# One square root for the head norms of two chunks, and the gate's tanh traced next to the decay's, in an RWKV-7 and Conformer step

## The chip, the cores and the metric

The kernel runs on one core of one Trainium2 chip, in one launch. Its time is device time in microseconds (us). Of the core's engines five appear here: TensorE (PE in the profile, with PEld for its weight loads) multiplies matrices, VectorE (DVE) and ScalarE (ACT) work element by element, GpSimd (POOL) does the same and issues transfers, SyncE (SP) issues transfers.

## The reference

One step of a hybrid decoder of two layers over 16 meta tokens, 1024 prompt tokens and 8 decode tokens (1048 columns), 1024 features wide. Layer 0 mixes tokens by a causal Conformer convolution, layer 1 by RWKV-7 with 16 heads of 64; each is followed by a squared-ReLU MLP of 4096. The change lies in layer 1. Cut to what matters:

```python
def _rwkv7(h, shift_prev, S0, x_mix, ...):
    ...
    r = xr @ w_r; k = xk @ w_k; v = xv @ w_v
    w_log = -softplus(-(w0 + tanh(xw @ w1) @ w2)) - 0.5
    decay = exp(-exp(w_log))
    a = sigmoid((a0 + (xa @ a1) @ a2))
    g = sigmoid(xg @ g1) @ g2
    kk = k * k_k;  kk = kk / max(sqrt(sum(kk * kk, per head)), L2_EPS)
    ...
    S_final, ys = lax.scan(_wkv7_step, S0, xs)
    y = moveaxis(ys, 0, 1)
    mu = mean(y, per head)
    var = mean(square(y - mu), per head)
    yn = (y - mu) * rsqrt(var + GN_EPS)
    yn = yn * gn_g + gn_b
    bonus = sum(r * k * r_k, per head) * v
    out = ((yn + bonus) * g) @ w_o
```

## The kernel before

Features lie on the 128 partitions in eight blocks, tokens along the free axis. Layer 0 and its MLP come first. Layer 1's mixer runs over four groups of tokens (`G1`: 272, 256, 256 and 264 columns). `mixer_in(g, tick)` loops over the eight feature blocks p (each of two heads): the projection r, the gate's second matrix, the decay and a (a tanh of each), the projection v, then a scan and products on DVE that make the operands of the recurrence. Ahead of the loop stand two narrow matmuls for the group: `gate` (tile lg, sigmoid written as a tanh) and, at p = 0, `decay_rate` (tile lwa).

The recurrence itself goes over 17 chunks of 64 tokens, the first of them the meta tokens. `front(c)` makes the products of a chunk (tiles A, nr, no), `chunk(c)` goes on with gg, bT, W, U, S and Y; Y is copied to a tile `ey`. `inverses` solves small triangular systems on DVE in many short steps (tiles tt and ni, one pair of instructions a step). All this is fed in between the projections: at each call of `tick` the generators of the inverses, of the recurrence and of `norm_gate` advance by a step.

`norm_gate` is the function that the change is about. It takes chunks in pairs (c, c + 1), c = 1, 3, ..., 15. For each chunk `stats` normalises 64 tokens x 16 heads, which lie as 128 partitions x 8 heads x 64: sum over a head (DVE, `ems`), centring (DVE), Square (ACT, `eq`), sum (DVE), Sqrt of 128x8 (ACT), reciprocal (DVE), and the multiplication of `ey` (DVE, 128x512). With a `yield` between, these are spread over ticks. Then, for each half of the features, PE transposes the pair (`yn`), ACT applies scale and bias (`ez`), DVE adds the bonus (`ebv`) and multiplies by the gate (`egt`), and the result is stored to a scratch `d_z`. At the end the 8 decode rows go the same way in two halves (`eyd`, `emsd`, `ynd`).

The Sqrt needs another table of functions in ACT than Tanh and Exp, so an `ACT_TABLE_LOAD` stands in ACT's queue wherever one follows the other. The key norms (`r16f`, one Sqrt a group) and the norms of the MLP layers are square roots as well.

What sets the order: each engine's instructions are put in order by a scheduler that simulates a timeline, with the code's order as the priority. PE is excepted in the mixer and in the tail: it keeps the order of the code. So are single instructions wrapped in `kept_place`, which keep their place among such on their engine.

After the mixer three tail groups (`G2`: 328, 352 and 352 columns) read `d_z`, multiply by w_o (`mixer_out`) and run layer 1's MLP (matmuls `ps_in` and `out`, additions to `h`) and the last norm. The first of them runs while the last chunks, the decode step and their norms are still being fed in.

Of the kernel before, what the change touches and what calls it, by code (L numbers as in the profile page):

```python
# [11 lines left out]
AF = mybir.ActivationFunctionType  # L12
ALU = mybir.AluOpType
AX = mybir.AxisListType
PSUM = bass.MemoryType.PSUM

P = 128
D = 1024
KT = D // P
# [3 lines left out]
DEC = 8  # L23
# [4 lines left out]
HS = 64  # L28
# [18 lines left out]
def hybrid_step(tc, x_prompt, x_sample, state_conv, state_shift, state_wkv, meta_tokens,  # L47
# [8 lines left out]
    nc = tc.nc  # L56
    ctx = ExitStack()
    with ctx:
# [8 lines left out]
        eps_t = consts.tile([P, 4], F32, name="eps_t")  # L67
# [39 lines left out]
        for name, ap in vecs:  # L107
            n = ap.shape[0]
# [28 lines left out]
        kept_place = tc.keep_in_program_order  # L137
# [258 lines left out]
        with ExitStack() as l0:  # L396
# [16 lines left out]
            h = {}  # L413
# [341 lines left out]
        for i, op in enumerate((ALU.is_gt, ALU.is_ge)):  # L755
            v = m_ar[:HS, i * HS:(i + 1) * HS]
# [210 lines left out]
        def mixer_in(g, tick):  # L967

            c0, n = G1[g]
# [42 lines left out]
            lg = lorap.tile([P, N1], F32, name=nm("lg"), tag="lg")  # L1012

            def decay_rate(ws):
                ps = narrow(ws, "wa")
                nc.scalar.activation(lwa[HALF[0], :n], ps[HALF[0]], AF.Tanh)
                nc.scalar.copy(lwa[HALF[1], :n], ps[HALF[1]])

            def gate(ws):
                ps = bank(nm("p", "g"))[:, :n]  # L1020
                for k in range(KT):
                    nc.tensor.matmul(ps, ws[k // HK][:, k % HK, :], mix(5, k), start=k == 0, stop=k == KT - 1)
                nc.scalar.activation(lg[:, :n], ps, AF.Tanh, scale=0.5)
                nc.scalar.activation(lg[:, :n], lg[:, :n], AF.Copy, scale=0.5, bias=0.5)

            def lora2(w, p, act, name):
                ps = bank(nm("l2", name))
# [15 lines left out]
            lumps = g == 2  # L1043
            spaced = (lambda: None) if lumps else both
            wg, ww = gate_w(), rate_w()
            gate(wg)
            act = mixed(0)
            carry["tail"]()
            act_v = mixed(3)
# [66 lines left out]
            for p in range(KT):  # L1116
                if p:
                    spaced()
                ps = proj(next(wrkv), act, n, nm("r", p), *((spaced, (3,)) if p else (first,)))
                rk2 = pr.tile([P, 2, N1], F32, name=nm("rk2", p), tag="rk2", bufs=2)  # L1120
                nc.scalar.copy(rk2[:, 1, :n], ps[:, :n])
                if p == 0:
                    decay_rate(ww)
                if g < 3:
                    for _ in keys_amid(p):
# [3 lines left out]
                ps = lora2(wg2, p, lg, f"g{p}")  # L1129
# [16 lines left out]
                ps = proj(next(wrkv), act_v, n, nm("v", p), spaced, (3,))  # L1146
# [114 lines left out]
        n_ = lambda shape, name, c, tag=None, bufs=1: wn.tile(shape, F32, name=f"{name}{c}", tag=tag or name, bufs=bufs)  # L1261
# [237 lines left out]
        def norm_gate():  # L1499

            KH = KT // 2
            fm = lambda t, n: t[:, :KH * n].rearrange("p (k t) -> p k t", k=KH)

            def stats(y, n, name):

                yv = y[:n].rearrange("t (h v) -> t h v", v=HS)
                ms = n_([P, 2, KT], "ems", name)
                sq = n_([P, KT * HS], "eq", name)
                over = lambda j: ms[:n, j].unsqueeze(2).broadcast_to([n, KT, HS])
                nc.vector.tensor_reduce(ms[:n, 0], yv, axis=AX.X, op=ALU.add)  # L1510
                nc.vector.scalar_tensor_tensor(yv, over(0), -1.0 / HS, yv, op0=ALU.mult, op1=ALU.add)
                yield 1
                kept_place(nc.scalar.activation(sq[:n], y[:n], AF.Square))
                yield 1
                kept_place(nc.vector.tensor_reduce(ms[:n, 1], sq[:n].rearrange("t (h v) -> t h v", v=HS), axis=AX.X, op=ALU.add))
                yield 1
                kept_place(nc.scalar.activation(ms[:n, 1], ms[:n, 1], AF.Sqrt, scale=1.0 / HS, bias=eps_t[:n, 2:3]))
                yield 1
                kept_place(nc.vector.reciprocal(ms[:n, 1], ms[:n, 1]))
                nc.vector.tensor_mul(yv, yv, over(1))  # L1520

            def load_rest(hf, lo, n):

                two = [n_([P, KH * P], tag, f"{lo}_{hf}", bufs=b) for tag, b in (("ebv", 1), ("egt", 2))]
                for t, src in zip(two, (d_bv, d_g)):
                    nc.sync.dma_start(fm(t, n), src[:, hf * KH:(hf + 1) * KH, lo:lo + n])
                return two

            def gated(pt, hf, lo, n, bv, gt):

                z = n_([P, KH * P], "ez", f"{lo}_{hf}", "eq")
                yield 0.5
                for k in range(KH):
                    p = hf * KH + k
                    kept_place(nc.scalar.activation(z[:, k * n:(k + 1) * n], pt[:, k * n:(k + 1) * n], AF.Identity, scale=vec("gn_g", p), bias=vec("gn_b", p)))
                w = KH * n
                yield 1
                kept_place(nc.vector.tensor_add(bv[:, :w], z[:, :w], bv[:, :w]))
                nc.vector.tensor_mul(gt[:, :w], bv[:, :w], gt[:, :w])
                yield 1  # L1540
                kept_place(nc.sync.dma_start(d_z[:, hf * KH:(hf + 1) * KH, lo:lo + n], fm(gt, n)))

            for c in range(1, NCH, 2):
                for i in range(2):
                    while st["done"] < c + i:
                        yield 1
                    yield from stats(ys[c + i], P, c + i)
                lo = META + (c - 1) * HS
                for hf in range(2):
                    rest = load_rest(hf, lo, P)  # L1550
                    yield 3
                    if not hf:
                        yield 1
                        yield 1
                    pt = bank(f"yn{c}_{hf}", "w")
                    to = pt.rearrange("p (j a u t) -> p j a u t", a=2, u=2, t=HS)
                    for j in range(2):
                        for i in range(2):
                            nc.tensor.transpose(to[:, j, :, i, :], ys[c + i][:, (2 * hf + j) * P:(2 * hf + j + 1) * P], ident)
                    yield from gated(pt, hf, lo, P, *rest)  # L1560
                st["free"] = c + 1
                st["normed"] = c + 1
            while not st["decoded"]:
                yield 1
            y8 = [n_([P, KT * HS], "ey", f"d{hf}", bufs=3) for hf in range(2)]
            for hf in range(2):
                nc.sync.dma_start(y8[hf][:DEC], d_y[:, hf * KH * P:(hf + 1) * KH * P])
            rest = load_rest(0, NP_TOK, DEC)
            yield 4
            for hf in range(2):  # L1570
                yield from stats(y8[hf], DEC, f"d{hf}")
            for hf in range(2):
                if hf:
                    rest = load_rest(hf, NP_TOK, DEC)
                    yield 3
                pt = bank(f"ynd_{hf}", "w")
                for k in range(KH):
                    nc.tensor.transpose(pt[:, k * DEC:(k + 1) * DEC], y8[hf][:DEC, k * P:(k + 1) * P], ident[:DEC, :DEC])
                yield from gated(pt, hf, NP_TOK, DEC, *rest)
            st["normed"] = NCH  # L1580
# [220 lines left out]
```

## Time and profile before

| | before |
|---|---|
| runs | 2641.32, 2638.36, 2640.5 us; median 2640.5 |
| the profiled execution | 2641.17 us, its span 2639.5 us |
| mean granted clock of TensorE | 0.993 |
| ACT_TABLE_LOAD of the head norms (L1517) | 9, of 1283 ns |
| ACT_TABLE_LOAD of the blocks' tanh (L1144) | 6, of 1283 ns |
| ACT_TABLE_LOAD of the key norms (L958) and of the decay's tanh (L1016) | 4 and 4, of 1283 ns |
| ACT_TABLE_LOAD of the gate's tanh (L1023) | 3, of 1283 ns |

The profile is of one execution. A row of the timeline gives the start and the duration in us, engine, line, operation, the tiles out<-in, and in brackets how long the engine idled before it and what ended that. A row of the groups gives the busy time and the mean duration in ns, then the idle time before and its releaser. A row of the windows gives a stretch, its length, the busy time of PE, PEld, DVE, ACT and POOL in it (with the instructions), the granted clock of TensorE (1.00 is full speed), and the DMA engines' busy share and GB/s. In the span, the gates' tanh of the four groups start from 1115.4 to 1550.4 us, the reciprocals of the head norms from 1376.0 to 1912.8, those of the decode rows at 2058.7 and 2064.5.

### The profile page before, as it was taken

The numbers are of one execution on the slowest core, as the hardware profiler recorded it, in microseconds if no ns is written. First come the engines' busy times: TensorE is split into PE (matmuls) and PEld (weight loads), VectorE is DVE, ScalarE is ACT, GpSimd is POOL, SyncE is SP. The second block draws the span as 40 slices with busy tenths as digits, with TensorE's granted clock in tenths as the row PEclk, the third lists the DMA queues.
The fourth block names the chain that finished last, engine by engine and source line by source line (L and its number), as shares of the span: only waits on it lengthen the run. The fifth ranks groups of instructions, "written<-read, shape, count | busy, mean of one in ns | idle before, by whom it ended". The sixth has DMA issues, their size and how long they took to land.

```text
span 2639.5 us, 51709 instructions
## 1 busy us (share of the span) xinstructions
PE 2584.5 (98%) x19956; PEld 2439.1 (92%) x19956; DVE 1720.5 (65%) x3610; ACT 1129.0 (43%) x2093; POOL 1453.0 (55%) x2060
## 2 busy tenths in 40 slices
PE   9999999999999999999999999999999999999998
PEld 8999999999999999877787877799999999999998
DVE  6999999997544444544867567686689544444435
ACT  5546435444534333233344545555444542222223
POOL 7677878878878777122111213476588763333331
PEclk9999999999999999999999999999999999999999
DMA  6663544554446543678876867898575542222211
GB/s 189 174 164 111 163 142 132 161 171 137 142 137 179 157 137 119 181 202 205 227 191 191 217 170 189 217 206 195 149 215 174 147 132 68 69 72 64 73 49 45
DMA packets 602060, 400.24 MB, mean 152 GB/s; under 512 B 96128, under 2 KB 548928, under 8 KB 601814
## 3 DMA queue, kind: packets, MB, share of 16 engines
q1 hardware_dynamic: 573764, 360.08, 49.7%
q0 software_dynamic: 8720, 26.35, 3.2%
q10 hardware_dynamic: 19330, 10.49, 1.4%
q8 instruction: 158, 2.59, 0.4%
q14 instruction: 88, 0.72, 0.1%
HBM read 338.94 MB, written 58.83 MB: 151 GB/s over the span
## 4 chain that ended last, share of the span: by engine, by line
PE 86%; DVE 8%; DMA 2%; ACT 2%; issue 1%; POOL 0%; ACTq 0%; SPq 0%; DVEq 0%; POOLq 0%
PE ps_in L190 8%; PE ps_in L192 8%; PE ps_in L191 8%; PE out L190 8%; PE out L191 8%; PE out L192 8%; PE pk L922 4%; PE pr L922 4%; PE pv L922 3%; PE ps_g L190 1%; PE ps_o L192 1%; PE ps_g L191 1%; PE ps_g L192 1%; PE ps_oo L190 1%; PE ps_o L190 1%
## 5 line engine op out<-in xcount | busy, mean ns | idle before, releaser
L165 POOL TENSOR_TENSOR wo_lo<-wo_raw,wo_hi 128x256 fp32r<-128x256 f32 x736 | 541.9, 769 | 286.2 <-ACT wo_hi L158 282.4
L165 POOL TENSOR_TENSOR wi_lo<-wi_raw,wi_hi 128x256 fp32r<-128x256 f32 x640 | 473.5, 772 | 241.7 <-ACT wi_hi L158 241.1
L190 PE MATMUL out<-hh,wo_hi 128*128 128x352 f32 (+2 forms) x1536 | 497.6, 324 | 10.5 <-DVE h L360 8.9
L360 DVE TENSOR_TENSOR h<-h,out 128x352 f32<-128x352 f32 (+2 forms) x768 | 386.7, 512 | 167.1 <-PE out L192 165.7
L190 PE MATMUL ps_in<-m_h,wi_hi 128*128 128x352 f32 (+2 forms) x1536 | 493.9, 322 | 0.0
L192 PE MATMUL ps_in<-m_l,wi_hi 128*128 128x352 f32 (+2 forms) x1536 | 492.7, 321 | 0.7 <-DVE m_l L288 0.7
L191 PE MATMUL out<-hh,wo_lo 128*128 128x352 f32 (+2 forms) x1536 | 492.5, 321 | 0.0
L191 PE MATMUL ps_in<-m_h,wi_lo 128*128 128x352 f32 (+2 forms) x1536 | 491.5, 320 | 0.0
L192 PE MATMUL out<-hl,wo_hi 128*128 128x352 f32 (+2 forms) x1536 | 490.8, 320 | 0.0
L542 DVE SCALAR_TENSOR_TENSOR cv<-u,wdw,cv 128x348 f32<-128x348 f32 (+2 forms) x720 | 378.9, 578 | 0.7
L158 ACT CAST wi_hi<-wi_raw 128x1024 fp32r<-128x1024 f32 x160 | 167.6, 1048 | 386.9 <-PE out L192 194.6
L158 ACT CAST wo_hi<-wo_raw 128x1024 fp32r<-128x1024 f32 x184 | 192.6, 1048 | 313.0 <-PE out L192 166.6
L190 PEld LDWEIGHTS out<-hh,wo_hi 128*128 128x128 f32 x1536 | 289.1, 188 | 16.4 <-DVE h L360 11.7
L190 PEld LDWEIGHTS ps_in<-m_h,wi_hi 128*128 128x128 f32 x1536 | 289.2, 188 | 1.5
L192 PEld LDWEIGHTS ps_in<-m_l,wi_hi 128*128 128x128 f32 x1536 | 288.2, 188 | 2.0 <-DVE m_l L288 1.5
L191 PEld LDWEIGHTS out<-hh,wo_lo 128*128 128x128 f32 x1536 | 288.5, 188 | 0.8
L191 PEld LDWEIGHTS ps_in<-m_h,wi_lo 128*128 128x128 f32 x1536 | 288.5, 188 | 0.6
L192 PEld LDWEIGHTS out<-hl,wo_hi 128*128 128x128 f32 x1536 | 288.2, 188 | 0.0
L347 DVE SCALAR_TENSOR_TENSOR ps_in<-ps_in,rs_m 128x352 f32<-128x352 f32 (+2 forms) x192 | 100.6, 525 | 256.1 <-PE ps_in L192 255.7
L142 DVE TENSOR_TENSOR hl<-ps_in,hh 128x352 fp32r<-128x352 f32 (+2 forms) x192 | 98.9, 515 | 124.0 <-ACT hh L141 123.9
L348 ACT ACTIVATE ps_in<-ps_in 128x352 f32<-128x352 f32 (+2 forms) x192 | 85.1, 444 | 129.5 <-DVE ps_in L347 129.3
L1099 POOL DMA_DIRECT2D d_n<-n x32 | 24.4, 762 | 189.1 <-DVE n L1089 97.6
(371 smaller groups left out, 4735.1 us busy)
## 6 DMA issues: line engine op xcount, KB each, us to landing
wi_raw<-in_w_mlp_in_dram SPq DMA_DIRECT2D x160, 512.0 KB
wo_raw<-in_w_mlp_out_dram SPq DMA_DIRECT2D x160, 512.0 KB
wk_raw<-in_rwkv_w_k_dram SPq DMA_DIRECT2D x32, 512.0 KB
wr_raw<-in_rwkv_w_r_dram SPq DMA_DIRECT2D x32, 512.0 KB
wv_raw<-in_rwkv_w_v_dram SPq DMA_DIRECT2D x32, 512.0 KB
d_ab<-ab POOLq DMA_DIRECT2D x32, 512.0 KB, 4.5
pg_raw<-in_conv_w_pw_dram SPq DMA_DIRECT2D x24, 512.0 KB
pa_raw<-in_conv_w_pw_dram SPq DMA_DIRECT2D x24, 512.0 KB
```

The costliest lines, as they stand in the source:

```text
L142: return eng_lo.tensor_sub(lo, src, hi.bitcast(F32))
L158: cast = nc.scalar.copy(hi[:, :a * b], raw[:, :a * b])
L165: eng_lo.tensor_sub(lo[:, cs], raw[:, cs], hi[:, cs].bitcast(F32))
L190: nc.tensor.matmul(ps, w[0], act[0], start=first, stop=False)
L191: nc.tensor.matmul(ps, w[1], act[0], start=False, stop=False)
L192: nc.tensor.matmul(ps, w[0], act[1], start=False, stop=last)
L347: nc.vector.scalar_tensor_tensor(s, s, 0.0, rs()[:, :n], op0=ALU.max, op1=ALU.mult)
L348: nc.scalar.activation(s, s, AF.Square)
L360: total = nc.vector.tensor_add(hv[:, 4 * i + m, :], hv[:, 4 * i + m, :], ps[:, :n])
L542: nc.vector.scalar_tensor_tensor(acc[m][:, :n], ug[:, m, j:j + n], wdw[:, m, j:j + 1], acc[m][:, :n], op0=ALU.mult, op1=ALU.add)
L922: nc.tensor.matmul(ps[:, :n], w[:, k, :], act[k], start=k == 0, stop=k == KT - 1)
L1099: nc.gpsimd.dma_start(d_n[ch0:ch0 + ncg, p].rearrange("c r t -> r c t"), n32[:, :ncg])
```

## The change

`stats` is split. `centred` does a chunk's sum, centring, Square and sum; it writes into one tile `ems` of 16 columns for the pair. `scaled` then does one Sqrt and one reciprocal for the 16 columns and the two multiplications. A pair takes seven steps up to there and not eight. The decode rows' two halves are joined in the same way (five steps, not eight). In `mixer_in`, `gate` issues its matmuls and returns a function `squash`, the Tanh and the scaling of lg; it is called at p = 0 right ahead of `decay_rate`, behind the copy of the first r block.

```diff
@@ gate @@
-                nc.scalar.activation(lg[:, :n], ps, AF.Tanh, scale=0.5)
-                nc.scalar.activation(lg[:, :n], lg[:, :n], AF.Copy, scale=0.5, bias=0.5)
+
+                def squash():
+                    nc.scalar.activation(lg[:, :n], ps, AF.Tanh, scale=0.5)
+                    nc.scalar.activation(lg[:, :n], lg[:, :n], AF.Copy, scale=0.5, bias=0.5)
+                return squash
...
-            gate(wg)
+            squash = gate(wg)
...
                 if p == 0:
+                    squash()
                     decay_rate(ww)
@@ norm_gate @@
-            def stats(y, n, name):
+            def centred(y, n, ms, name):
...
-                ms = n_([P, 2, KT], "ems", name)
+                mean, power = ms
                 sq = n_([P, KT * HS], "eq", name)
-                over = lambda j: ms[:n, j].unsqueeze(2).broadcast_to([n, KT, HS])
-                nc.vector.tensor_reduce(ms[:n, 0], yv, axis=AX.X, op=ALU.add)
-                nc.vector.scalar_tensor_tensor(yv, over(0), -1.0 / HS, yv, op0=ALU.mult, op1=ALU.add)
+                nc.vector.tensor_reduce(mean[:n], yv, axis=AX.X, op=ALU.add)
+                nc.vector.scalar_tensor_tensor(yv, mean[:n].unsqueeze(2).broadcast_to([n, KT, HS]), -1.0 / HS, yv, op0=ALU.mult, op1=ALU.add)
                 yield 1
                 kept_place(nc.scalar.activation(sq[:n], y[:n], AF.Square))
                 yield 1
-                kept_place(nc.vector.tensor_reduce(ms[:n, 1], sq[:n].rearrange("t (h v) -> t h v", v=HS), axis=AX.X, op=ALU.add))
+                kept_place(nc.vector.tensor_reduce(power[:n], sq[:n].rearrange("t (h v) -> t h v", v=HS), axis=AX.X, op=ALU.add))
+
+            def scaled(ys_, n, power):
+
+                kept_place(nc.scalar.activation(power[:n], power[:n], AF.Sqrt, scale=1.0 / HS, bias=eps_t[:n, 2:3]))
                 yield 1
-                kept_place(nc.scalar.activation(ms[:n, 1], ms[:n, 1], AF.Sqrt, scale=1.0 / HS, bias=eps_t[:n, 2:3]))
-                yield 1
-                kept_place(nc.vector.reciprocal(ms[:n, 1], ms[:n, 1]))
-                nc.vector.tensor_mul(yv, yv, over(1))
+                kept_place(nc.vector.reciprocal(power[:n], power[:n]))
+                for i, y in enumerate(ys_):
+                    yv = y[:n].rearrange("t (h v) -> t h v", v=HS)
+                    nc.vector.tensor_mul(yv, yv, power[:n, i * KT:(i + 1) * KT].unsqueeze(2).broadcast_to([n, KT, HS]))
...
@@ the pairs of chunks @@
-                    yield from stats(ys[c + i], P, c + i)
+                    if i == 0:
+                        ms = n_([P, 2, 2 * KT], "ems", c)
+                    yield from centred(ys[c + i], P, [ms[:, j, i * KT:(i + 1) * KT] for j in range(2)], c + i)
+                    yield 1
+                yield from scaled([ys[c], ys[c + 1]], P, ms[:, 1])
@@ the decode rows @@
+            ms = n_([P, 2, 2 * KT], "ems", "d")
             for hf in range(2):
-                yield from stats(y8[hf], DEC, f"d{hf}")
+                yield from centred(y8[hf], DEC, [ms[:, j, hf * KT:(hf + 1) * KT] for j in range(2)], f"d{hf}")
+            yield from scaled(y8, DEC, ms[:, 1])
```

The order of the instructions at three places follows, before and after. The first is ACT's queue around the gate of group 3 (lg3, from the matmul p3_g), with the key norm r16f3, the first r block rk23_0 and the decay lwa behind it. Before:

```order
L1023 ACT_TABLE_LOAD
L1023 ACTIVATE lg3_17290<-p3_g_17303 128x264
L1072 COPY vt2_7_17349<-vt2_7_17348 128x256
L1024 ACTIVATE lg3_17290<-lg3_17290 128x264
L1073 DMA d_v_76<-vt2_7_17349 128x2x128
L1372 COPY p646_17237<-po6_17425 32x8x32 x2
L958 ACT_TABLE_LOAD
L958 ACTIVATE r16f3_17454<-r16f3_17454 128x66
L1121 COPY rk23_0_17474<-pr3_0_17397 128x264
L1016 ACT_TABLE_LOAD
```

After:

```order
L1025 ACTIVATE lg3_17281<-p3_g_17294 128x264
L1075 COPY vt2_7_17338<-vt2_7_17337 128x256
L1026 ACTIVATE lg3_17281<-lg3_17281 128x264
L1076 DMA d_v_76<-vt2_7_17338 128x2x128
L1376 COPY p646_17231<-po6_17414 32x8x32 x2
L958 ACT_TABLE_LOAD
L958 ACTIVATE r16f3_17443<-r16f3_17443 128x66
L1124 COPY rk23_0_17463<-pr3_0_17386 128x264
L1016 ACT_TABLE_LOAD
```

The Tanh of lg3 stands where it stood, two table loads ahead of lwa; the load ahead of it is gone, as the Sqrt of chunk 5's norm that came before it (ems5) is now done together with chunk 6's. The gates of groups 0 to 2 stand in their old places too.

The second is DVE's queue ahead of the copy of U of chunk 3 (uv): the inverses of group 2 (ni5, tt5), the bonus addition of chunks 1 and 2 (ebv16_0) and the operands of block 2 (rk2_2, ab2_2). Before:

```order
L1250 TENSOR_TENSOR ni5_15439<-ni5_15439,tt5_13_15994 128x13x18
L1155 SCALAR_TENSOR_TENSOR rk22_2_15852<-st2_2_14513,negs_12332,pb2_2_16006 128x256
L1249 TENSOR_TENSOR tt5_12_15997<-ni5_15439 128x228
L1176 TENSOR_TENSOR wa2_2_15859<-rk22_2_15852,wa2_2_15859 128x256
L1187 TENSOR_TENSOR ab2_2_16021<-rk22_2_15852,ex2_2_16012 128x4x128
L1250 TENSOR_TENSOR ni5_15439<-ni5_15439,tt5_12_15997 128x12x19
L1538 TENSOR_TENSOR ebv16_0_15781<-ez16_0_15938,ebv16_0_15781 128x512
L1188 TENSOR_TENSOR ab2_2_16021<-wa2_2_15859,em2_2_16010 128x4x128
L1380 COPY uv_12362<-U3_16036 64x8x64
```

After:

```order
L1159 SCALAR_TENSOR_TENSOR rk22_2_15849<-st2_2_14513,negs_12332,pb2_2_16003 128x256
L1253 TENSOR_TENSOR tt5_13_15991<-ni5_15434 128x234
L1180 TENSOR_TENSOR wa2_2_15856<-rk22_2_15849,wa2_2_15856 128x256
L1191 TENSOR_TENSOR ab2_2_16018<-rk22_2_15849,ex2_2_16009 128x4x128
L1254 TENSOR_TENSOR ni5_15434<-ni5_15434,tt5_13_15991 128x13x18
L1192 TENSOR_TENSOR ab2_2_16018<-wa2_2_15856,em2_2_16007 128x4x128
L1384 COPY uv_12362<-U3_16033 64x8x64
L1354 TENSOR_SCALAR p644_16319<-p324_15928,par32q_12280 128x8x32 x2
L1253 TENSOR_TENSOR tt5_12_15994<-ni5_15434 128x228
```

The inverses are one step (tt5_12 and its ni5) behind at the copy of uv, and the addition to ebv16_0 stands behind it. Further up in the queue chunk 1's multiplication of ey, which stood among earlier work, is now right ahead of chunk 2's.

The third is DVE's queue in the tail: the decode rows (emsd, eyd0, eyd1) among the MLP's additions to h1_0 of the first tail group (out1_14) and the split of the next group's d_z (z1_l). Before:

```order
L1510 TENSOR_REDUCE emsd0_24013<-eyd0_23955 8x8
L142 TENSOR_TENSOR hl10_30_23777<-ps_in1_30_0_23778,hh10_30_23776 128x328
L347 SCALAR_TENSOR_TENSOR ps_in1_31_0_23829<-ps_in1_31_0_23829,rs_m10_20132 128x328
L142 TENSOR_TENSOR z1_l4_24117<-zr14_24142,z1_h4_24109 128x352
L142 TENSOR_TENSOR z1_l5_24118<-zr14_24142,z1_h5_24110 128x352
L360 TENSOR_TENSOR h1_0_19336<-h1_0_19336,out1_14_0_0_23867 128x328
L1511 SCALAR_TENSOR_TENSOR eyd0_23955<-emsd0_24013,eyd0_23955 8x512
L360 TENSOR_TENSOR h1_0_19336<-h1_0_19336,out1_14_0_1_23875 128x328
L142 TENSOR_TENSOR z1_l6_24119<-zr16_24148,z1_h6_24111 128x352
L360 TENSOR_TENSOR h1_0_19336<-h1_0_19336,out1_14_0_2_23883 128x328
```

After:

```order
L1513 TENSOR_REDUCE emsd_23989<-eyd0_23931 8x8
L142 TENSOR_TENSOR hl10_30_23753<-ps_in1_30_0_23754,hh10_30_23752 128x328
L347 SCALAR_TENSOR_TENSOR ps_in1_31_0_23805<-ps_in1_31_0_23805,rs_m10_20116 128x328
L1513 TENSOR_REDUCE emsd_23989<-eyd1_23932 8x8
L142 TENSOR_TENSOR z1_l4_24090<-zr14_24115,z1_h4_24082 128x352
L142 TENSOR_TENSOR z1_l5_24091<-zr14_24115,z1_h5_24083 128x352
L360 TENSOR_TENSOR h1_0_19321<-h1_0_19321,out1_14_0_0_23843 128x328
L1514 SCALAR_TENSOR_TENSOR eyd0_23931<-emsd_23989,eyd0_23931 8x512
L360 TENSOR_TENSOR h1_0_19321<-h1_0_19321,out1_14_0_1_23851 128x328
L142 TENSOR_TENSOR z1_l6_24092<-zr16_24121,z1_h6_24084 128x352
L1514 SCALAR_TENSOR_TENSOR eyd1_23932<-emsd_23989,eyd1_23932 8x512
L360 TENSOR_TENSOR h1_0_19321<-h1_0_19321,out1_14_0_2_23859 128x328
```

The reduction and the centring of the second half (emsd from eyd1, eyd1) have come in among the additions; before they stood behind all those of out1_14.

## The prediction

> **What bounds the kernel now.** I read the page's busy times and its chain of waits first.
>
> ```profile
> PE 2584.5 (98%) x19956; PEld 2439.1 (92%) x19956; DVE 1720.5 (65%) x3610; ACT 1129.0 (43%) x2093; POOL 1453.0 (55%) x2060
> PE 86%; DVE 8%; DMA 2%; ACT 2%; issue 1%; POOL 0%; ACTq 0%; SPq 0%; DVEq 0%; POOLq 0%
> ```
>
> TensorE (PE) works 2584.5 of 2639.5 us; it is idle for 55.0 us in all. ScalarE (ACT) is idle for more than half of the span and holds 2% of the chain. The change takes work from ACT and a little from VectorE (DVE). It leaves every matmul. So it can pay only where PE is waiting, or where PE's clock is lowered. I went on to the groups of ACT and DVE, then to each idle stretch of PE near a moved instruction.
>
> ```profile
> L1517 ACT ACT_TABLE_LOAD x9 | 11.5, 1283 | 1.0 <-ACT vt L1072 0.9
> L1023 ACT ACT_TABLE_LOAD x3 | 3.8, 1283 | 0.1
> L1517 ACT ACTIVATE ems<-ems,eps_t 128x8 f32<-128x8 f32 x16 | 4.8, 301 | 4.2 <-DVE ems L1515 3.6 <-ACT dst L1466 0.4
> ```
>
> Each table load takes 1.283 us, each head-norm Sqrt 0.301.
>
> **What goes: ACT's time.** By the instruction order, ACT's table loads go from 43 to 35. Those of the norms of chunks 1, 3, 5 and 7, of the gates of groups 2 and 3, and two returns to tanh (fourth feature block of groups 2 and 3, counted from 0) are gone. One more, of chunk 9, only changes its place: it moves ahead of the next layer's own square root. Eight of the sixteen Sqrts go, and one of the two for the decode rows. ACT has 8 x 1.283 + 9 x 0.301 = 10.3 + 2.7 = 13.0 us less to do. What covered these loads?
>
> ```profile
> 1547.15 1.28 ACT L1023 ACT_TABLE_LOAD   x1
> 1550.38 0.39 ACT L1023 ACTIVATE lg<-p_g 128x264 f32<-128x264 f32 x1 [1.95 <-PE p_g L1022]
> ...
> 1645.48 1.28 ACT L1144 ACT_TABLE_LOAD   x1 [0.51 <-PE l_a L1138]
> 1646.78 0.48 ACT L1144 ACTIVATE wa<-l_w,half 128x264 f32<-128x264 f32 x1
> ...
> 1650.02 0.37 ACT L1148 COPY vv<-pv 128x264 f32<-128x264 f32 x1
> 1650.44 0.39 PE L814 MATMUL pb<-r,hspread 128*128 128x264 f32 x1 [0.23 <-ACT vv L1148]
> ...
> 1470.00:1510.00 40.00, 40.00 (x531) 33.30 (x531) 18.66 (x39) 21.23 (x50) 6.54 (x10) 1.00 0.78 205
> ```
>
> The load for group 3's gate ends at 1548.43, and ACT then idles 1.95 us for the gate's matmuls: it was loaded early, in time nobody wanted. This is the usual case: ACT waits for PE, not PE for ACT. The return to tanh at 1645.48 is the one place where ACT was late: ACT ran on without a pause to the copy of vv, and PE waited 0.23 us for that. Without the load ACT is 1.28 us earlier there, and 0.23 us of PE's idle time goes. The rest I cost at nothing: PE's own work hides them, as in the window from 1470 to 1510, where PE is busy for all of its 40.00 us while ACT returns to tanh for group 2's fourth block. Where PE's cover is thinner than it looks, their removal gains; it can't lose. The term is **-0.23**, and the far bound, all of ACT's time back, is -13.0.
>
> The Trainium skill ("ScalarE: Activation LUTs", "What ACT_TABLE_LOAD costs") puts a change of table at about 1.28 us of load and 1.38 us of drain, 2.66 us together; by it the far bound would be an estimate of 8 x 2.66 + 2.7 = 24.0 us. The trace agrees on the load and shows no drain: the next ACTIVATE starts 1.30 us after the load does (1645.48 to 1646.78).
>
> **The tanh half.** In the order the gate's tanh stands where it stood, in all four groups: ahead of the square root of the key norms (r16f), not beside the decay's tanh. The scheduler puts ACT's instructions by its own timeline, so the later place in the code moves nothing; the gate's load in groups 2 and 3 goes because the head norm's Sqrt ahead of it went. Its cost is 0, from either side.
>
> **What moves on DVE.** The multiplication of the first chunk of a pair now stands right ahead of that of the second. The first of three places where this meets a waiting PE is the copy of U of chunk 3.
>
> ```profile
> 1440.23 0.39 DVE L1250 TENSOR_TENSOR ni<-ni,tt 128x228 f32<-128x228 f32 x1
> 1440.54 0.69 DVE L1538 TENSOR_TENSOR ebv<-ez,ebv 128x512 f32<-128x512 f32 x1
> 1441.14 0.69 DVE L1188 TENSOR_TENSOR ab<-wa,em 128x512 f32<-128x512 f32 x1
> 1441.74 0.68 DVE L1380 COPY uv<-U 64x512 f32<-64x512 f32 x1
> ...
> 1443.09 0.66 PE L1559 MATMUL yn<-ident,ey 128*128 128x128 f32 x4 [3.17 <-ACT uv L1381]
> ```
>
> DVE is busy without a pause up to the copy (1441.74), and PE waits 3.17 us. In such a full stretch a 512-wide operation comes 0.60 us after the one ahead (1440.54, 1441.14, 1441.74) and a step of the inverse 0.31 (1440.23 to 1440.54). The order now has one pair of inverse steps (2 x 0.31) and the addition to ebv (0.60) behind the copy, and chunk 1's multiplication (0.60) ahead of it: -0.62 - 0.60 + 0.60 = **-0.6** (0 if PE finds another wait right behind it).
>
> The second is chunk 7's Y.
>
> ```profile
> 1604.05 1.15 PE L1397 MATMUL Y<-sv,xa 128*64 128x64 f32 x32 [0.94 <-DVE nr L1297]
> 1615.50 1.06 PE L1338 MATMUL gg<-x,no 32*32 32x32 f32 x32 [3.04 <-ACT em L1159]
> ```
>
> Ahead of the masks (nr) that Y waits for stands one more multiplication (+0.60), and two inverse steps fewer (-0.62): 0 there. If these did not give way it would be +0.60. At 1615.50 a step that stood ahead of the last mask goes, about **-0.2** (0.31 less the overlap; bounds -0.3 and 0).
>
> The third is the decode rows, beside the MLP of the first tail group.
>
> ```profile
> 2044.13 0.43 PE L190 MATMUL out<-hh,wo_hi 128*128 128x328 f32 x1 [0.91 <-DVE hl L142]
> 2045.68 0.80 DVE L1511 SCALAR_TENSOR_TENSOR eyd<-emsd,eyd 8x512 f32<-8x512 f32 x1
> 2045.81 0.41 PE L190 MATMUL out<-hh,wo_hi 128*128 128x328 f32 x1 [0.50 <-DVE h L360]
> ...
> 2061.33 0.67 DVE L1511 SCALAR_TENSOR_TENSOR eyd<-emsd,eyd 8x512 f32<-8x512 f32 x1
> ```
>
> The first half's centring (2045.68) is in the way already: PE waits 0.91 and 0.50 us for additions to h. The second half's reduction and its centring, at 2061.33 before, now stand among the same additions, since nothing between them is left to wait for. Each takes about 0.60 in a full stretch, and the queue's later rows (the additions to h, which free PE's banks) come that much later: **+1.2**, with ends 0 (the banks give slack) and +1.2. I take the upper end, because PE is waiting there in the row.
>
> The transposes yn of chunk pairs 7 and 11 come a step earlier on PE and could meet an ey that isn't ready.
>
> ```profile
> 1653.62 0.69 DVE L1520 TENSOR_TENSOR ey<-ey,ems 128x512 f32<-128x512 f32 x1
> 1662.36 0.66 PE L1559 MATMUL yn<-ident,ey 128*128 128x128 f32 x4
> ```
>
> Chunk 8's ey is ready at 1654.3, one 0.60 later now; the transposes go some 3.7 us ahead (the eight matmuls of half a projection and what stands with them), to 1658.7. No wait: 0. GpSimd's store of the inverses goes a few us later and SP's loads swap places, each far ahead of its reader: 0.
>
> The sum: -0.23 - 0.6 - 0.2 + 1.2 = +0.2 us. The terms' ends give -1.1 to +1.8. The profiled execution took 2641.17 us, 0.67 above the median of the runs; on the median the sum gives 2640.7.
>
> **What a wait costs beside itself: the clock.** A wait of a few us can halve PE's clock after it. The windows give the granted clock in the last column but two:
>
> ```profile
> 1440.00:1442.00 2.00, 0.00 (x0) 0.00 (x0) 2.00 (x5) 0.00 (x0) 0.11 (x1) 1.00 0.10 33
> 1582.00:1584.00 2.00, 0.46 (x2) 0.46 (x3) 1.94 (x6) 0.00 (x0) 0.19 (x1) 0.50 0.57 97
> 1586.00:1588.00 2.00, 2.00 (x6) 1.49 (x6) 1.90 (x5) 0.00 (x0) 1.13 (x3) 0.50 0.89 203
> 1616.00:1618.00 2.00, 1.89 (x28) 1.78 (x25) 2.00 (x7) 1.13 (x4) 0.25 (x2) 0.50 0.24 59
> 1620.00:1622.00 2.00, 2.00 (x6) 1.38 (x6) 0.00 (x0) 0.00 (x0) 0.59 (x1) 0.50 1.07 239
> 1702.00:1704.00 2.00, 2.00 (x17) 1.78 (x16) 1.25 (x5) 0.84 (x2) 0.67 (x1) 0.50 0.72 198
> ```
> ```profile
> 1583.54 1.12 PE L1356 MATMUL bT<-ident,bk 128*128 128x128 f32 x4 [3.31 <-DVE nr L1297]
> 1584.45 5.50 PE L922 MATMUL pr<-mx,wr_raw 128*128 128x264 f32 x16
> 1650.72 3.83 PE L922 MATMUL pr<-mx,wr_raw 128*128 128x264 f32 x16
> 1700.11 1.54 PE L1379 MATMUL U<-w,p 64*64 64x64 f32 x32 [1.95 <-DVE w L1365]
> ```
>
> After the gaps of 3.31 us (1583.54), 3.04 (1615.50) and 1.95 (1700.11) the clock is 0.50; the first two stretches last about 6 us and cost half of that, 3.0 each (the 16 matmuls of pr at 1584.45 take 5.50 where 3.83 is usual). The gap of 3.17 us ahead of 1443.09 left it at 1.00. So length alone doesn't decide, and near 2 to 3 us a small shift of a gap can win or lose 3 us. The range rests on this.
>
> **The rivals.** Likeliest, 0.40: the stretches of 0.50 stay as they are, give or take one, and the sum holds: 2640.7, its own range 2637.0 to 2645.0 (the sum's ends, and one stretch of 3.0 won or lost).
>
> Faster by the clock, 0.24: the gaps shift or shrink so that two stretches of 0.50 go. For: the gaps at 1443 and 1615 get 0.6 and 0.2 shorter, and 3.17 us once passed unpunished. Against: the gaps at 1583 and 1700 have no moved row ahead of them that would shorten them. Price: 2 x 3.0 + the 1.2 if the decode term is hidden: 2640.7 - 6.0 - 1.2 = 2633.5. The Trainium skill ("TensorE: Matmul & The Clock Gate", "What's actually happening") says that activity is judged in free-running windows of 3.413 us, so that the drop depends on where a gap lies in a window; the trace agrees so far, with 3.17 us that cost nothing and 1.95 that did. By it the waits could stay as they are and the penalties still be dealt anew. The same page ("HAM oscillation — how this bites in real kernels") asks for no idle gaps above about 3.4 us; the trace is against that as a safe limit, since gaps of 1.95 and 3.04 us were enough.
>
> Slower, 0.28: DVE work moved into stretches where DVE is full makes PE's gaps longer until they lower the clock. Places: Y of chunk 7, 0.94 us before, and the additions at 2044, 0.91. With the multiplication not offset, and both decode rows ahead of one addition, these become about 1.5 and 2.1 us; from about 1.95, the shortest gap in the rows that was followed by 0.50, the clock falls. For: DVE is the releaser of both. Against: the offsets in the order, and that DVE's load there is a few us only. Price: 0.6 + 2 x 3.0 on the sum: 2640.7 + 6.6 = 2647.3.
>
> ACT's time all on the path, 0.08: then 2640.7 - 13.0 = 2627.7. For: 1650.44, where PE waits for ACT. Against: 0.23 us is all that is seen of it, and 2% ACT in the chain.
>
> **The numbers.** A measurement of this kernel can tell about 0.2%, 5.3 us. Against the median of 2640.5, faster by more than that (below 2635.2) are the second and fourth cases, 0.24 + 0.08 = 0.32; the likeliest case lies within, 0.40; the third is above 2645.8, 0.28. The forecast is the likeliest, 2640.7. The range goes from 2631.0 (the second case with another stretch of 3.0, less half a us) to 2648.0 (the third with 0.7 for its ends); it leaves out the fourth case and the edges of the two others.
>
> **What would show it.** Right: ACT busy about 13 us less, near 1116, and PE's busy time unchanged but for the clock; the gap ahead of yn of chunk 1 near 2.6 instead of 3.17; PE's waits on h near 2044 to 2046 longer by about a us; the stretches of 0.50 near 1584, 1616 and 1702 still there. Wrong: the span shorter by 10 us or more with the clock as it is (then ACT bound somewhere that the rows don't show); another count of half-clock stretches (then the clock, not the sum, set the result); a gap that ACT ends at a norm's Sqrt, now behind two chunks.

## The result and the profile after

The changed kernel takes 2646.91 us in the median of 14 runs (2645.58 to 2654.2), the kernel before 2641.02 (2638.22 to 2645.77, 14 runs): 5.9 us more, ratio 1.0023, 95% interval 1.0016 to 1.003. The profiled execution has a span of 2645.7 us against 2639.5, 6.2 more, of which PE's idle time is 4.4 (59.4 against 55.0) and its busy time 1.8. The first lines are the page's busy times and chain, then the groups of the norms' and the gate's loads on ACT.

```profile
PE 2586.3 (98%) x19956; PEld 2440.8 (92%) x19956; DVE 1719.4 (65%) x3601; ACT 1116.4 (42%) x2076; POOL 1458.0 (55%) x2060
PE 83%; DVE 10%; DMA 2%; issue 2%; ACT 2%; POOL 1%; SPq 0%; ACTq 0%; DVEq 0%; POOLq 0%
...
L1522 ACT ACT_TABLE_LOAD x4 | 5.1, 1283 | 0.5 <-ACT vt L1075 0.4
L1522 ACT ACTIVATE ems<-ems,eps_t 128x16 f32<-128x16 f32 x8 | 2.5, 308 | 1.6 <-DVE ems L1518 1.2 <-ACT dst L1470 0.4
L1025 ACT ACT_TABLE_LOAD x1 | 1.3, 1283 | 0.0
```

ACT has 12.6 us less to do (1129.0 to 1116.4), the loads of the norms went from 9 to 4 and those of the gates from 3 to 1. None of it shortened the span; in the chain DVE has 10% where it had 8.

I laid PE's timelines of before and after over each other, row by row. The changed kernel is 4.5 us ahead at 1721 us. Most of that lead is not the change's: 0.8 us of it stands at 1370, ahead of the first moved instruction (1373.50 before), and from there to 1721 it spends 6.7 us less at a clock of 0.50, which at half speed is an estimated 3.3 us. What the change itself gives there is small: it waits less at the copy of U of chunk 3 and at pb, and more at Y. It is level at 1810, 2.1 us behind at 1941, 4.0 at 2130, and 6.2 at the end. PE's rows at the places that the prediction names:

```profile
1441.48 0.89 PE L1570 MATMUL yn<-ident,ey 128*128 128x128 f32 x4 [2.19 <-ACT uv L1385]
...
1604.58 1.15 PE L1401 MATMUL Y<-sv,xa 128*64 128x64 f32 x32 [1.28 <-DVE nr L1301]
1615.93 1.06 PE L1342 MATMUL gg<-x,no 32*32 32x32 f32 x32 [2.94 <-ACT ez L1542]
...
1648.55 0.48 PE L814 MATMUL pb<-r,hspread 128*128 128x264 f32 x1
...
1748.00 1.16 PE L1291 MATMUL A<-xa,bk 64*128 64x128 f32 x14 [1.42 <-DVE fs L1409]
1794.51 1.13 PE L1291 MATMUL A<-xa,bk 64*128 64x128 f32 x14 [2.71 <-DVE nr L1301]
...
1938.71 0.43 PE L190 MATMUL out<-hh,wo_hi 128*128 128x328 f32 x1 [2.00 <-DVE h L360]
...
2046.30 0.42 PE L190 MATMUL out<-hh,wo_hi 128*128 128x328 f32 x1 [0.93 <-DVE hl L142]
2048.57 0.42 PE L190 MATMUL out<-hh,wo_hi 128*128 128x328 f32 x1 [1.10 <-DVE h L360]
2051.83 0.42 PE L190 MATMUL out<-hh,wo_hi 128*128 128x328 f32 x1 [0.90 <-DVE h L360]
```

The wait at 1794.51 is the one that grew most, and the prediction does not have it. Before, it was 0.69 us, and chunk 12's sum and centring came behind the masks nr that the matmuls wait for:

```profile
1795.39 1.13 PE L1287 MATMUL A<-xa,bk 64*128 64x128 f32 x14 [0.69 <-DVE nr L1297]
...
1795.49 0.41 DVE L1297 TENSOR_TENSOR nr<-A,m_ar 128x256 f32<-128x256 f32 x1
1795.82 0.18 DVE L1519 RECIPROCAL ems<-ems 128x8 f32<-128x8 f32 x1
1796.04 0.69 DVE L1520 TENSOR_TENSOR ey<-ey,ems 128x512 f32<-128x512 f32 x1
1796.77 0.69 DVE L1510 TENSOR_REDUCE ems<-ey 128x8 f32<-128x512 f32 x1
1797.49 1.09 DVE L1511 SCALAR_TENSOR_TENSOR ey<-ems,ey 128x512 f32<-128x512 f32 x1
```

After, they stand ahead of the masks (DVE's rows of the changed kernel):

```profile
1790.07 0.68 DVE L1513 TENSOR_REDUCE ems<-ey 128x8 f32<-128x512 f32 x1
...
1791.66 1.08 DVE L1514 SCALAR_TENSOR_TENSOR ey<-ems,ey 128x512 f32<-128x512 f32 x1
...
1794.61 0.41 DVE L1301 TENSOR_TENSOR nr<-A,m_ar 128x256 f32<-128x256 f32 x1
```

In the code chunk 12's sum always followed chunk 11's reciprocal and multiplication. These used to wait for a Sqrt, and the sum waited with them; now the reciprocal is behind both chunks, nothing holds the sum back, and it comes 1.7 us of DVE's work too early.

The last term is a surprise: from 2130 us on PE has one wait in either kernel, of 0.14 us near the end, and yet the changed one falls 2.2 us further behind. The windows of 300 us show it in the count of matmuls. Before:

```profile
2200.00:2500.00 300.00, 300.00 (x1874) 300.00 (x1873) 120.65 (x232) 75.09 (x120) 110.10 (x156) 1.00 0.23 69
```

After:

```profile
2200.00:2500.00 300.00, 300.00 (x1864) 300.00 (x1863) 119.73 (x231) 75.08 (x119) 108.98 (x155) 1.00 0.23 69
```

The clock is 1.00 in both and PE is busy for all of it, but ten matmuls fewer fit: the mean time from one start to the next (the pitch) is 161.1 ns against 160.3. Nothing in the order differs there.

### The profile page after: what moved, and what is told of

Same layout as the page of the kernel before. It is cut to its first block, busy times and chain, and to the rows that moved or that the text cites. A ratio compares the mean times of both kernels' runs of the same rounds, so it can differ in the third digit from the quotient of the medians.

```text
span 2645.7 us, 51683 instructions
## 1 busy us (share of the span) xinstructions
PE 2586.3 (98%) x19956; PEld 2440.8 (92%) x19956; DVE 1719.4 (65%) x3601; ACT 1116.4 (42%) x2076; POOL 1458.0 (55%) x2060
## 4 chain that ended last, share of the span: by engine, by line
PE 83%; DVE 10%; DMA 2%; issue 2%; ACT 2%; POOL 1%; SPq 0%; ACTq 0%; DVEq 0%; POOLq 0%
PE ps_in L192 8%; PE ps_in L190 8%; PE ps_in L191 8%; PE out L190 8%; PE out L191 8%; PE out L192 8%; PE pk L922 4%; PE pr L922 4%; PE pv L922 3%; PE ps_o L192 1%; PE ps_o L190 1%; PE ps_o L191 1%; PE ps_g L190 1%; PE ps_g L191 1%; PE ps_g L192 1%
```

## The experiments

Theory after the result: the loss is the sum of three independent things, (a) DVE rows of the chunk pairs that come ahead of what PE waits for, (b) the same for the decode rows, (c) the place in memory, since the tile `ems` is 64 bytes a partition wider (2 x 16 columns, not 2 x 8) and what is allocated behind it moves. Rivals: the table loads pay and only the decode rows lose; the tail's pitch is an accident of one execution. The first four are set against 2641.47 us (35 runs of before), the next three (the changed kernel with the narrow tile, all sums held, more table loads) and the second profile of the eight steps against 2642.04 (23 runs), and the three after them against 2641.42 (27 runs). The ratio is an estimate over all the runs and can differ from the quotient of two medians by 0.0004.

**Only the wider tile.**

```diff
-                ms = n_([P, 2, KT], "ems", name)
+                ms = n_([P, 2, 2 * KT], "ems", name)[:, :, :KT]
```

> The kernel before, with the tile ems as wide as in the changed kernel (16 columns, of which 8 are used): every engine's instructions stand in the same order as before. Two theories on the last 460 us, where the changed kernel's matmuls follow each other every 161.1 ns and those of before every 160.3, with no wait on either side (2.2 us together). Layout: the tile is 64 bytes a partition wider, and what lies behind it in the memory moves; then this run is about 2.2 us slower (ratio 1.0008) with a pitch of 161.1 ns. Accident of one execution: ratio 1.0000 within 0.0005 and a pitch that may be either.

Measured: 2643.06 us, ratio 1.0009 (1.0000 to 1.0017). The window, in a kernel whose order is that of before:

```profile
2200.00:2500.00 300.00, 300.00 (x1864) 300.00 (x1863) 120.96 (x233) 75.12 (x119) 108.72 (x154) 1.00 0.23 69
```

It is 1864, as in the changed kernel. Over all the runs told here, the eight profiles with a tile of the old width or 128 bytes more have 1873 or 1874 matmuls (160.3 ns), all six with 64 bytes more have 1864 (161.1 ns). The accident is out, and so is a difference between chips, since one of the six and three of the eight are of the same chip. The time alone (1.6 us in the medians, with an interval that starts at 1.0000) would not show it. That it is the place of what lies behind the tile is argued: nothing else differs in the order, but no run moved one such tile by itself.

**Only the decode rows** (`ems` in the wide form; the pairs use the old `stats`).

> Only the decode rows' two halves share one square root (tile ems as wide as in the changed kernel); the chunk pairs stay as before. Order theory: the second half's reduction and centring come in ahead of additions to h that PE waits for, and PE's waits near 2044 to 2052 grow from 0.9 + 0.5 to about 0.9 + 1.1 + 0.9 us: 1.5 us slower, ratio 1.0006. If the layout of the memory costs 2.2 us more, 1.0014. Rival, that the loss lies in the chunk pairs: 1.0000.

Measured: 2644.99 us, 1.0014 (1.0005 to 1.0022): 1.9 us over the wide tile alone. PE's rows in this run:

```profile
2043.83 0.42 PE L190 MATMUL out<-hh,wo_hi 128*128 128x328 f32 x1 [0.93 <-DVE hl L142]
2046.10 0.42 PE L190 MATMUL out<-hh,wo_hi 128*128 128x328 f32 x1 [1.10 <-DVE h L360]
2049.36 0.42 PE L190 MATMUL out<-hh,wo_hi 128*128 128x328 f32 x1 [0.91 <-DVE h L360]
```

The waits are 0.93 + 1.10 + 0.91 = 2.94 us where before had 0.91 + 0.50 = 1.41: 1.5 us, the same as in the full change.

**Only the chunk pairs**, in seven steps.

> Only the chunk pairs share one square root, in seven steps; the decode rows and the gate's tanh stay as before. Order theory: the changed kernel's lead of 4.5 us at 1721 is gone by 1940 (chunk 12's centring ahead of the masks of chunk 13 alone costs 1.7), so the pairs by themselves come out 1 to 2 us slower, ratio 1.0004 to 1.0008; with the layout's 2.2 us, 1.0015. Rival, that the eight table loads saved pay and the decode rows alone lose: faster by 1 to 4 us, 0.9985 to 0.9996.

Measured: 2645.10 us, 1.0014 (1.0006 to 1.0023): 2.0 us over the wide tile alone. The three parts add up in the medians: 1.6 (tile) + 1.9 (decode) + 2.0 (pairs) = 5.5 of the change's 5.9 us; each of them is uncertain by about 2 us, so the sum says that no large part is missing, and the rows say where each lies.

**The pairs in eight steps**, so that PE's order is that of before:

```diff
                     yield from centred(ys[c + i], P, [...], c + i)
                     yield 1
+                    if i == 0:
+                        yield 1
```

> The chunk pairs share one square root, but a pair takes eight steps as before (an empty step between its two chunks), and the decode rows stay as before: PE's order is that of before, row for row, and the same table loads are gone. Order theory: chunk 12's centring still stands ahead of the masks of chunk 13, since the multiplication of chunk 11 that held it back is now behind it; so a wait of about 2.7 us near 1794 stays, and the ratio lies from 0.9995 to 1.0008. If it was PE's earlier transposes (pairs 7 and 11) that cost time, this one is 1 us or more faster than the run with seven steps.

Measured: 2643.99 us, 1.0008 (1.0000 to 1.0017), wide tile included. PE's transposes are in their old places, and the wait is still there:

```profile
1792.55 1.13 PE L1287 MATMUL A<-xa,bk 64*128 64x128 f32 x14 [2.65 <-DVE nr L1297]
```

So it is the order on DVE, not the earlier step, that makes it. The difference of 1.1 us to the seven steps is within the intervals. The rows do tell the two apart: all three profiles of kernels with seven steps have a wait of 0.35 us at Y near 1683 and one of 0.48 to 0.50 at out near 1806, and no other profile has either. So the dropped step costs about 0.8 us by the rows. A second profile of the same kernel (with the wide tile) gave 2646.41 us, and a wait of 2.73 us at 1795.02:

> A second look at the pairs in eight steps with the wide tile, in the same chip's series: one profile more. Order theory: again a wait of about 2.7 us near 1793, a pitch of 161.1 ns in the last group, and the wait near 1936 at either 1.1 or 2.0 us.

The wait near 1936 is 2.00 us there, at 1941.14. It is 1.13 in before and 2.01 in the run with only the wider tile, whose rows stand in the same order: this one varies from execution to execution, and the 0.87 us by which it grew in the changed kernel (2.00 at 1938.71) is not shown to be the change's.

**The changed kernel with the narrow tile** (mean and power share 8 columns, order unchanged).

```diff
-                        ms = n_([P, 2, 2 * KT], "ems", c)
+                        ms = n_([P, 2 * KT], "ems", c)
-                    ... [ms[:, j, i * KT:(i + 1) * KT] for j in range(2)] ...
+                    ... [ms[:, i * KT:(i + 1) * KT]] * 2 ...
```

> The changed kernel with the tile ems as wide as before (64 bytes a partition: the mean and the power of a chunk share their 8 columns); every engine's instructions stand in the order of the changed kernel. Layout theory: the pitch of the last group's matmuls goes back from 161.1 to 160.3 ns and 2.2 us of the changed kernel's loss go: 2644.5, ratio to before 1.0014. Rival, that the whole loss is of the order and the wider tile's run was chance: as the changed kernel, 1.0023.

Measured: 2644.27 us, 1.0012 (1.0003 to 1.0021), against 1.0023 with the wide one. The window has 1874 matmuls again. The two intervals overlap, so the times don't say how much of the loss was 64 bytes; by the rows it is 2.2 of the 5.9 us, by the run with only the wider tile 1.6.

**All second chunks' sums held** to their place in the code on DVE (eight steps, narrow tile, decode rows as before; `held` is `i == 1`, the second chunk of a pair).

```diff
-                nc.vector.tensor_reduce(mean[:n], yv, axis=AX.X, op=ALU.add)
+                (kept_place if held else lambda i: i)(nc.vector.tensor_reduce(mean[:n], yv, axis=AX.X, op=ALU.add))
```

> The chunk pairs share one square root in eight steps, the tile is as wide as before, and the second chunk's reduction is held to its place in the code on DVE, so that its centring stands behind the masks (for chunk 12: behind those of chunk 13, as before the change). Decode rows as before. Order theory: the wait near 1794 is back to about 0.7 us (2.0 us less than in the eight steps without it), the pitch is 160.3 ns (2.2 us less), so 4.2 us off that run's 2644.0: 2639.8, ratio 0.9993, from 0.9985 to 1.0003. Rival, that sharing the square root has a cost of its own: 1.0005 or more.

Measured: 2644.49 us, 1.0010 (1.0002 to 1.0019): a miss by 4.7 us. The wait near 1794 did shrink, but new ones took its place (ACT's rows, then PE's):

```profile
1420.81 0.63 ACT L1512 ACTIVATE eq<-ey 128x512 f32<-128x512 f32 x1 [7.14 <-DVE ey L1510]
1421.46 0.37 ACT L1148 COPY vv<-pv 128x256 f32<-128x256 f32 x1
...
1421.89 0.39 PE L814 MATMUL pb<-r,hspread 128*128 128x256 f32 x1 [1.47 <-ACT vv L1148]
...
1759.39 0.42 PE L192 MATMUL ps_in<-m_l,wi_hi 128*128 128x328 f32 x1 [0.57 <-DVE m_l L288]
...
1797.70 1.13 PE L1287 MATMUL A<-xa,bk 64*128 64x128 f32 x14 [1.15 <-DVE nr L1297]
```

Chunk 2's centring, held, comes later; its Square stands in ACT's queue ahead of the copy of vv and idles 7.14 us for it, so vv is late and PE waits for vv, 1.47 us. Near 1759 PE waits 0.74 and 0.57 us for m_l; what makes it late was not followed. The three are 2.8 of the 4.7 us, and the rest is open.

**More table loads**: before, with a Sqrt of one column ahead of each Square.

```diff
+                kept_place(nc.scalar.activation(ms[:n, 1, 0:1], eps_t[:n, 2:3], AF.Sqrt))
                 kept_place(nc.scalar.activation(sq[:n], y[:n], AF.Square))
```

> The kernel before, with one more Sqrt of one column ahead of each Square of the head norms (its result is overwritten): six more table loads and 18 short Sqrts, about 6 x 1.28 + 18 x 0.3 = 13 us more for ACT, as much as the change takes from it. PE's order is that of before; DVE's differs in two small places. Order theory: ACT's time is off the path but for one place (0.23 us before), so 0 to 1.5 us slower, ratio 1.0000 to 1.0006. Rival, that ACT's time counts in full: 13 us, 1.0049.

Measured: 2653.11 us, 1.0046 (1.0033 to 1.0058). The expectation of 0 to 1.5 us failed; ACT is busy 9.4 us more (1138.4) and the kernel is 11 us slower. ACT's and PE's rows at the fourth block of group 3 show the largest piece:

```profile
1649.88 1.28 ACT L1513 ACT_TABLE_LOAD   x1
...
1652.41 1.28 ACT L1159 ACT_TABLE_LOAD   x1
1653.70 0.42 ACT L1159 ACTIVATE em<-wa 128x264 f32<-128x264 f32 x1
...
1654.57 0.37 ACT L1148 COPY vv<-pv 128x264 f32<-128x264 f32 x1
...
1654.99 0.59 PE L814 MATMUL pb<-r,hspread 128*128 128x264 f32 x1 [3.19 <-ACT vv L1148]
```

A load between a block's tanh and its exp, and the one back, stand ahead of the copy of vv, and PE waits 3.19 us. The same happens at 1370.67, where PE waits 1.67 us for vv and before not at all. Beyond the 0.23 us of before the two make 4.6 of the 8.8 us by which this profile is longer; it also spends 6.8 us more at 0.50 (an estimated 3.4 us), and the waits at Y and U near 1610 and 1705 grew, which I did not separate. The Squares stand there; the eight loads that the change took away stood, but for one, where ACT soon idled 0.58 to 2.70 us for PE. So "ACT has time to spare" was true of the places from which the loads went, and not of ACT.

**Only chunk 12 held** (eight steps, narrow tile, decode rows as before; `held` is `c + i == 12`).

> The chunk pairs share one square root in eight steps, the tile is as wide as before, the decode rows as before, and of all centrings only chunk 12's is held to its place on DVE, so that it stands behind the masks of chunk 13. Order theory: the wait near 1794 is about 0.7 us and not 2.7; the pitch of the last group is 160.3 ns; no waits of 1 us or more at 1422 and 1758, which the run with all centrings held had. Against the eight steps with the narrow tile (next run but one) 2.0 us less: about 2639.8, ratio to before 0.9993, from 0.9985 to 1.0002. Rival, that the norms' merged multiplications have another cost that the profiles don't show as a wait: 1.0005 or more.

Measured: 2639.84 us, 0.9991 (0.9982 to 0.9999), as expected; that it agrees to the tenth is luck, as the runs tell some 2 us. The wait is 1.1 us and not the 0.7 expected:

```profile
1791.16 1.13 PE L1287 MATMUL A<-xa,bk 64*128 64x128 f32 x14 [1.12 <-DVE nr L1297]
```

**Only the pairs of chunks 1 and 7** (eight steps, narrow tile).

```diff
+                    if c not in (1, 7):
+                        yield from stats(ys[c + i], P, c + i)
+                        continue
```

> Only the pairs of chunks 1 and 7 share one square root (eight steps, narrow tile); those are the two at which every merged run showed a gain (1.0 us at the copy of U of chunk 3, 0.2 to 0.7 us at pb near 1650). Four table loads fewer than before, and no moved row near 1794 or in the tail. Order theory: 1.2 to 1.7 us faster, ratio 0.9994, from 0.9986 to 1.0002. Rival, that the gaps that get shorter are made up by the next wait: 1.0000 to 1.0005.

Measured: 2638.77 us, 0.9991 (0.9982 to 1.0000), inside the expected range and at the edge of what the runs can tell from none. PE's rows at the two gains, where yn waits 2.19 us and pb not at all:

```profile
1438.55 0.66 PE L1590 MATMUL yn<-ident,ey 128*128 128x128 f32 x4 [2.19 <-ACT uv L1381]
...
1643.66 0.48 PE L814 MATMUL pb<-r,hspread 128*128 128x264 f32 x1
```

**Eight steps with the narrow tile**, the control of the two.

> The pairs in eight steps as in the run of that name, but with the tile as wide as before; row for row the same order on every engine. Layout theory: pitch 160.3 ns and 2.2 us less than the run with the wide tile: 2641.8, ratio 1.0000 (0.9993 to 1.0008). Order theory: the wait of about 2.7 us near 1794 stays.

Measured: 2642.77 us, 1.0007 (0.9998 to 1.0016); the wait of chunk 13 is still there, and behind it the clock falls:

```profile
1795.51 1.13 PE L1287 MATMUL A<-xa,bk 64*128 64x128 f32 x14 [2.66 <-DVE nr L1297]
...
1798.00:1800.00 2.00, 2.00 (x9) 2.00 (x8) 0.29 (x1) 0.00 (x0) 0.00 (x0) 0.50 1.24 198
```

Against it, holding the one sum is worth 2.9 us, with an uncertainty of about 2; the two orders differ in eight neighbouring places on DVE and nowhere else. The wait itself gives 1.5 of it. The wait near 1936 is 0.53 us in both kernels that hold chunk 12's sum and 1.13 to 2.01 in all others, which may be a part of the gain; two profiles don't show it.

The stretch at 0.50 points to a further cost of this wait. Behind the wait near 1794, of 2.51 to 2.73 us in six profiles, the clock falls in four; behind 0.66 to 1.15 us, in the other eight, it never does.

**A tile 128 bytes wider**, in before.

> The kernel before with the tile ems 128 bytes a partition wider (24 columns, 8 used), where the first such run had 64; row for row the order of before. If it is the place modulo 128 bytes of what lies behind the tile that counts, the pitch of the last group is 160.3 ns as before; if it is any shift, or the size of it, 161.1 ns or another value.

One run took 2645.26 us, against 2642.05 for one run of before; single runs of before alone differ by more, so only the window is read. It has 1873 matmuls, a pitch of 160.3 ns.

```profile
2200.00:2500.00 300.00, 300.00 (x1873) 300.00 (x1872) 120.64 (x232) 75.15 (x119) 110.35 (x156) 1.00 0.23 69
```

So it is not any shift, nor its size; 0, 64 and 128 bytes agree with a rule of the place modulo 128, though three points do not prove one.

## Why the prediction was right or wrong

The measured 2646.91 lies in the range, but not in the likeliest case: 5.9 us is past the 5.3 that I called the same, and the chance of 0.28 for slower came up, at places that it did not name. That its price, 2647.3, lies 0.4 us from the measured time is luck: it was made of one wait and two clock penalties, and the loss is made of a centring in the way at chunk 12, the decode rows and a wider tile. A slip in the sums beside that: the terms' ends and one stretch of 3.0 give the likeliest case 2636.4 to 2645.3, not 2637.0 to 2645.0.

- **ACT's time.** 13.0 us forecast, 12.6 measured, and by the rows nothing of it on the path but at pb: right. The -0.23 there was small: the 0.23 us wait is gone and PE gains 0.67 us there in the changed kernel (from the start of pv to the next l_g 8.58 us, 9.25 before) and as much, within 0.02, in the runs with pairs 1 and 7 merged. What was wrong is the reason given, that ACT has cover in general; the run with more loads shows that it has it by place.
- **The tanh half.** 0 forecast. It was not run by itself, but up to the decode rows the changed kernel and the run with only the chunk pairs, which leaves the Tanh alone, have the same order on PE, DVE, ACT and GpSimd. So the move did nothing there: right.
- **The copy of U of chunk 3.** -0.6 forecast, 3.17 to 2.19 us measured, -1.0. The gap got shorter, and yet in this execution a stretch of 0.50 followed it, which did not in the profile before:

```profile
1442.00:1444.00 2.00, 2.00 (x7) 1.59 (x6) 1.96 (x6) 0.00 (x0) 0.17 (x1) 0.50 0.64 223
```

  That is not the shorter gap's doing: 0.50 follows the 3.17 us in the run with only the decode rows too, and does not follow the 2.19 us in that with only chunk 12 held.

- **Y of chunk 7.** 0 forecast with an end of +0.6; 0.94 to 1.28 us, +0.3. At 1615, -0.2 forecast and 3.04 to 2.94 measured.
- **The decode rows.** +1.2 forecast, as the term's upper end; +1.5 by the waits. The mechanism and the place were right, the end was too low.
- **The transposes of pairs 7 and 11.** 0 forecast; the dropped step that brings them forward costs about 0.8 us at two small waits, of which the prediction has neither.
- **The step that failed** is the list of "three places where this meets a waiting PE". The reasoning used for the decode rows (a centring comes forward because nothing between is left to wait for) holds for every second chunk of a pair, and I did not follow it to chunk 12, where PE's wait for the masks of chunk 13 grew by 2.0 us (0.69 to 2.71). The run that holds this one sum, and its control, show the cause. Of the lead that PE had by then another 1.4 us went at 1748, for DVE's fs; the changed kernel with the narrow tile, in the same order, has no wait there, so that one is not shown to be the change's.
- **The term that was missing** is the tile's width: 2.2 us in a stretch that the change does not touch. No row of before could show it.
- **The clock rivals.** By the trace's clock record the kernel before has five stretches at 0.50 before the end, 30.7 us, of which the prediction's rows show three; the first two of these are 6.83 us long, at half speed 3.4 us each and not the 3.0 that I took, and the third 10.24. The changed kernel has seven, 30.7 us too, so the other count, which I had named as a sign that the clock set the result, says nothing by itself. Each is one, two or three times 3.41 us long. This is what the Trainium skill ("TensorE: Matmul & The Clock Gate", "What's actually happening") says of free-running windows of 3.413 us. The same gap going either way agrees with it: 3.17 us ahead of yn of chunk 1 left the clock at 1.00 in before and was followed by 0.50 in the run with the tile 128 bytes wider, whose order is the same. The equal sums are chance: over all fourteen profiles they go from 20.5 to 44.4 us, at half speed an estimated 10 to 22 us of time, which is a large part of why the runs of one kernel spread over 8 us. Over the runs, the mean granted clock is 0.9924 in the changed kernel (14 runs) and 0.9928 in before (the 85 runs beside the experiments), an estimated 1.3 us, uncertain by about 1.5. So neither rival's price came, but "no net change" is not shown either. At chunk 12 the third rival's mechanism is there: a gap that DVE's work makes longer, and behind it, in four of six profiles (not in the one of the changed kernel), the clock that falls, at a place that I had not named.

What stays open: which tiles of the last group the 64 bytes displace, whether and why their reads are slower there, and how much of the 5.9 us is the clock's.

## What to carry to other kernels

When a change takes an instruction out of a queue, ask of each one that stood behind it whether it was held back by the missing one, and follow all of its copies: work that comes forward on a busy engine lengthens the wait of whoever needs the next row. Cost an engine's time by place, with the row that waits for it, since ACT could give back 13 us for less than 1, while a kernel that gave it 9 more was 11 us slower. And keep a tile's size when only the order is to be changed, or run the size by itself.

## What the runs showed of the hardware

A scratch tile 64 bytes a partition wider, used by DVE and ACT only, slowed the matmuls of a later stretch from 160.3 to 161.1 ns each at a full clock, 0.5%, in all six profiles with it, and 128 bytes, in one profile, did not. Where it has nothing else to wait for, the next activation starts 1.30 us after a table load does (1645.48 to 1646.78 before). The removal of eight such loads shows in PE's rows at one place only, 0.67 us.
